# A decoder layer on one core: the norm's weight applied per partition behind the transposes, and four subtractions put behind the fifth product's addition

## The chip, the cores and the metric

The kernel runs on one core of a Trainium2 chip. It is one launch; the metric is the device time in microseconds of one execution, and of several executions the median counts. TensorE (PE in the profile) multiplies matrices, with its weight loads shown apart as PEld; VectorE is DVE, ScalarE is ACT, GpSimd is POOL, and SyncE is SP, which here issues nearly all DMAs. A line number such as L414 is a line of the kernel before. In the changed kernel the same statements stand a few lines further down.

## The reference

One layer of a decoder trunk over 1024 tokens of width 1024, in float32. Three parts follow each other, each adding to the residual stream `x`:

```python
def rms_norm(x, g):
    y = x * lax.rsqrt(jnp.mean(x * x, axis=-1, keepdims=True) + EPS)
    return y * g

def swiglu(h, w_gate, w_up, w_down):
    return (jax.nn.silu(h @ w_gate) * (h @ w_up)) @ w_down

x = x + 0.5 * swiglu(rms_norm(x, g_ffn1), w1_gate, w1_up, w1_down)    # hidden width 2816
h = rms_norm(x, g_mix)
proj = h @ w_in          # two token mixers with 8 heads of 64 each: sparse attention over the
...                      # top 256 keys with rotary positions, and stick-breaking attention
x = x + merged @ w_out
x = x + 0.5 * swiglu(rms_norm(x, g_ffn2), w2_gate, w2_up, w2_down)
```

The change is in how the two feed-forward parts (FFNs) get their normed input. `rms_norm` scales each row (token) by a number of its own and each column (feature) by `g`.

## The kernel before, in words

**Precision.** Every matrix product runs as three products of a reduced float32 type (fp32r): an operand is halved into a high part (a copy that rounds, on ScalarE, L377) and a low part (the operand less the high part, L378, on GpSimd or VectorE), and high times high, high times low and low times high are summed in PSUM. These are the matmul lines L497, L498 and L499 of an FFN's first half.

**An FFN's first half** (`ffn_in`) multiplies the normed input, as the right side, by gate and up weights, as the left side. It takes 2 by 2 blocks and a scheme with seven products in place of eight: the left sides are A11, A12, A22 and the sums S1 to S4, the right sides B11, B21, B22 and the sums T1 to T4 (each four tiles of 128x512 with its low halves beside it). T1 = B12 - B11, T2 = B22 - T1, T3 = B22 - B12, T4 = B21 - T2. Four banks of PSUM groups, with the letters a to d, take the products and the transposes in turn; a bank is free again when its last reader is done. The hidden width is walked in 11 pairs of blocks: the first pair by `opening`, all others by `products`. The second half (`ffn_out`) does the same with the down weights, and adds into `x`. FFN names begin with "a" in the first FFN, with "b" in the second.

**The right sides** are made by the class `Right`, the subject of the change. Its rows are the 128-token tiles of `x`, the first four (tokens 0 to 511) as one half, the last four as the other. `gain` loads `g` once, broadcast to all 128 partitions (128x1024). `stat` sums the squares of a tile on ScalarE (L408), computes the mean on VectorE (`ms`, L284) and the inverse root on GpSimd (`rs`, L286). `norm` multiplies a tile by `rs` (a value per partition) and by `g` (a value per column) in one VectorE instruction (L414), in two column halves for the first four tiles, whole for the last four. `turn` transposes the normed tiles on TensorE, four 128x128 pieces into a bank (L428), and halves the result from PSUM into a right side (ScalarE L377, VectorE L378); for B12 and B22 it also subtracts on VectorE to get T1, T3 and T2 (L431, L446). `keep` copies transposed values out of PSUM as they are, for later sums (L439 on VectorE, L441 on ScalarE), `less` subtracts lists (L446), and `low` halves T1 to T4 (L462 and L464).

**The order.** `opening` is written by hand: its instructions go to each engine in the order of the program. At its end stand, in this order, the sixth product into bank b, the halving of T3, `u2` plus that product (L617), four subtractions on VectorE for T4 (L446), the fifth product into bank d, `u3` = `u2` plus it (L622), the seventh product into bank c, the halving of T4, then the third product, which adds onto bank d, and the fourth onto bank c. Outside it a scheduler orders the instructions of each engine. In the second FFN the first two right sides are made while the output projection of the attention (`project`, matmul lines L308 to L310) still runs; it calls `between`, which turns B11 and B21. The attention in the middle is ordered by a planner of its own; the change does not alter that.

**The start.** SP issues the tiles x0 and x1, then `g`, x2 and x3, then the first gate weights `a0r` and up weights `a1r`. `gcolm`, a later load of another weight, already has the form that the change gives to `g`: eight rows of 128 are loaded, and turned into a value per partition and column tile.

Of the kernel before, what the change touches and what calls it, by code (L numbers as in the profile page):

```python
# [10 lines left out]
F32 = mybir.dt.float32  # L11
# [5 lines left out]
AF = mybir.ActivationFunctionType  # L17
ALU = mybir.AluOpType
# [5 lines left out]
P = 128  # L24
# [3 lines left out]
ND = D // P  # L28
# [3 lines left out]
HD = 64  # L32
# [25 lines left out]
def f32(ap):  # L58
    return ap.bitcast(F32)
# [186 lines left out]
def trunk(ctx, tc, x, positions, g_ffn1, w1_gate, w1_up, w1_down, g_mix, w_in, g_cq, w_uq_a, w_q_idx,  # L246
          g_q_a, g_k_a, w_uv_a, w_o_a, w_o_b, w_out, g_ffn2, w2_gate, w2_up, w2_down, inv_freq, out):
    nc = tc.nc
# [132 lines left out]
    class Right:  # L381
# [7 lines left out]
        def __init__(self, g, bank, gains, yt, ct, tt, ts, spare, nm):  # L389
            self.g, self.bank, self.gains, self.yt, self.ct = g, bank, gains, yt, ct  # L390
            self.tt, self.ts, self.spare, self.nm = tt, ts, spare, nm
            self.B, self.y, self.gB = {}, {}, None

        def gain(self):
            self.gB = self.gains(f"{self.nm}g")
            nc.sync.dma_start(self.gB, self.g[0].partition_broadcast(P))

        def place(self, xs, half, junk=None):

# [11 lines left out]
        def norm(self, t):  # L411
            xt = self.x[t]
            for c, out_ in ((slice(0, 1024), xt),) if self.half else ((HI, self.y[0, 0][t]), (LO, self.y[0, 1][t])):
                nc.vector.scalar_tensor_tensor(out_, xt[:, c], self.rs[t], self.gB[:, c], op0=ALU.mult, op1=ALU.mult)  # L414

        def operands(self, *ns):
            for n in ns:
# [2 lines left out]
        def turn(self, n, letters="abcd", less=None):  # L420

            if n not in self.B:
                self.operands(n)
            rows, out = self.y[self.ROWS[n]], []
            for k in range(4):
                ps = self.bank("pst", letters[k % len(letters)])
                for j in range(4):
                    nc.tensor.transpose(ps[:, j * P:(j + 1) * P], rows[j][:, k * P:(k + 1) * P], ident)  # L428
                halve(self.B[n][k], ps, nc.vector)
                if less:  # L430
                    nc.vector.tensor_sub(less[0][k], ps, less[1][k])  # L431
                out.append(ps)
            return out

        def keep(self, copies, eng=None):

            for t, ps in copies:
                if eng is nc.vector:
                    nc.vector.tensor_copy(t, ps)  # L439
                else:  # L440
                    nc.scalar.activation(t, ps, AF.Copy)  # L441

        def less(self, to, a, b):

            for t, p, q in zip(to, a, b):
                nc.vector.tensor_sub(t, p, q)  # L446

        def kept(self):

# [25 lines left out]
    def ffn_in(nm, R, wg, wu, raw, op, sums, ct, bank, staged, rows, first=None, beside=lambda n, ins: None):  # L475
# [54 lines left out]
        def opening(raws, rows, nxt):  # L530


            A = [dict(zip(("A11", "A12", "A21", "A22"), (r[:, q] for r in rs for q in (HI, LO)))) for rs in raws]
            O = ({}, {})

            def left(e, *names):
                for n in names:
                    O[e][n] = halve(op(f"{nm}{e}0{n}"), A[e][n])

            ps, sg = {}, {}  # L540

            def half(r, c, q, letter=None):

                if not q:
                    ps[r, c] = bank("pg", letter)
                times(O[0][f"A{r + 1}{q + 1}"], B[f"B{q + 1}{c + 1}"], ps[r, c], not q)

            def gate(r, c):
                sg[r, c] = ct(f"{nm}sg")
                nc.scalar.activation(sg[r, c], ps[r, c], AF.Silu)  # L550

            def up(n, ps_, start=True):
                a, b = FACTORS[n]
                times(O[1][a], B[b], ps_, start)

            if "B11" not in B:
                left(0, "A11")
                R.operands("B12", "B11", "B21", "B22", "T1")
                R.kept()
                copies = list(zip(R.raw["T3"], R.turn("B11")))  # L560
                left(0, "A12")
                R.keep(copies[0:1], nc.vector)
                p21 = R.turn("B21")
                R.kept2()
                copies += zip(R.raw["T4"], p21)
                left(0, "A21", "A22")
                R.second()
            else:
                copies = []
                R.operands("B22", "T1")  # L570
                left(0, "A11", "A12", "A21", "A22")
            for t, n in enumerate((("A11",), ("A12",), (), ())):
                R.keep(copies[1 + 2 * t:3 + 2 * t], nc.vector)
                if 4 - t <= len(rows):
                    R.stat(rows[t + len(rows) - 4])
                left(1, *n)
            r = R.raw
            r["T2"] = [R.spare(f"{nm}r22{k}") for k in range(4)]
            S = {n: sums(f"{nm}s{n}") for n in ("S1", "S2", "S3", "S4")}
            A11, A12, A21, A22 = (A[1][n] for n in ("A11", "A12", "A21", "A22"))  # L580
            nc.vector.tensor_add(S["S1"], A21, A22)
            nc.vector.tensor_sub(S["S2"], S["S1"], A11)
            A[1].update(S)
            for t in rows:
                R.norm(t)
            half(0, 0, 0, "a")
            half(0, 0, 1)
            gate(0, 0)
            left(1, "S2")
            half(1, 0, 0, "b")  # L590
            pa = bank("pa", "a")
            up(1, pa)
            u2 = ct(f"{nm}u2")
            half(1, 0, 1)
            nc.scalar.activation(u2, pa, AF.Copy)
            gate(1, 0)
            left(1, "S1")
            up(2, pa, False)
            R.turn("B12", "cdab", (r["T1"], r["T3"]))
            nc.gpsimd.tensor_sub(S["S3"], A11, A21)  # L600
            nc.gpsimd.tensor_sub(S["S4"], A12, S["S2"])
            left(1, "S3")
            R.less(r["T2"], R.turn("B22", "bcdc"), r["T1"])
            R.low("T1", nc.gpsimd)
            half(0, 1, 0, "d")
            half(1, 1, 0, "b")
            R.low("T2", nc.vector)
            left(1, "S4", "A22")
            half(0, 1, 1)
            gate(0, 1)  # L610
            half(1, 1, 1)
            gate(1, 1)
            R.less(r["T3"], r["T2"], r["T3"])
            pb = bank("pb", "b")
            up(6, pb)
            R.low("T3", nc.vector)
            nc.vector.tensor_add(u2, u2, pb)  # L617
            R.less(r["T4"], r["T4"], r["T2"])
            pd = bank("pd", "d")
            up(5, pd)  # L620
            u3 = ct(f"{nm}u3")
            nc.vector.tensor_add(u3, u2, pd)  # L622
            pc = bank("pc", "c")
            up(7, pc)
            R.low("T4", nc.vector)
            nc.vector.tensor_mul(sg[0, 0], sg[0, 0], pa)
            nc.vector.tensor_add(u3, u3, pc)
            nxt = nxt()
            up(3, pd, False)
            c12 = ct(f"{nm}c12")  # L630
            nc.vector.tensor_add(c12, u2, pd)
            up(4, pc, False)
            nc.vector.tensor_add(u2, u2, pc)
            return [sg[0, 0], sg[0, 1], sg[1, 0], sg[1, 1]], (None, c12, u2, u3), nxt
# [184 lines left out]
    with tc.tile_pool(name="ring1", bufs=1) as rpool, tc.tile_pool(name="s1", bufs=1) as spool, tc.tile_pool(name="ps1", bufs=1, space=PSUM) as psum:  # L819
# [3 lines left out]
        with tc.tile_pool(name="t1", bufs=1, side="right") as tpool, tc.tile_pool(name="c1", bufs=1) as cpool:  # L823
# [54 lines left out]
                rows(t)  # L878
            gcolm = column(g_mix, ND, "gcolm")
            gcolq = column(g_cq, QR // P, "gcolq")  # L880
            gk = cst.tile([P, HD], F32, name="gk")
            nc.sync.dma_start(gk, g_k_a[0].partition_broadcast(P))

            R.place(xs[0:4], 0)
            R.stat(0)
# [73 lines left out]
        h2, rows = [], []  # L959
# [68 lines left out]
    with ctxf, fp as fpool, psm as psum, tc.manual_schedule(  # L1028
# [384 lines left out]
        for w in ow.live:  # L1413
# [5 lines left out]
        rope, ropeq = s("rope", "rope", 2), s("ropeq", "rope", 2)  # L1419
        cos2, sin2, qcos, qsin = (t[:, j * 512:(j + 1) * 512].rearrange("p (t d) -> p t d", t=NT)  # L1420
                                  for t in (rope, ropeq) for j in range(2))
        cqh = [s(f"cqh{j}", "cqT", 4, F32R) for j in range(2)]
        cql = [s(f"cql{j}", "cqT", 4, F32R) for j in range(2)]
        KX, QI, WQ = {}, {}, {}
# [716 lines left out]
    with tc.tile_pool(name="ring2", bufs=1) as rpool, tc.tile_pool(name="ps6", bufs=1, space=PSUM) as psum:  # L2141
# [82 lines left out]
        with tc.tile_pool(name="c2", bufs=1) as cpool:  # L2224
            ct = of(cpool, "c", NC_, 512)
            x1 = residual(1)
            R = Right(g_ffn2, bank, fp(op), ct, ct, tt, ts, in_turn((sums, 3), (ct, 1)), "b")

            def between():
                R.operands("B12")  # L2230
                R.kept()
                R.kept2()
                R.keep(zip(R.raw["T3"], R.turn("B11")))
                R.keep(zip(R.raw["T4"], R.turn("B21")))

            R.gain()
            R.place(x0, 0)
            for t in range(4):
                R.stat(t)
                R.norm(t)  # L2240
            project(1, M1, x1, between)
            R.gain()
            R.place(x1, 1, sums)
            for t in range(3):
                R.stat(t)
                R.norm(t)

            ffn_in("b", R, w2_gate, w2_up, raw, op, sums, ct, bank, staged[1], [3])
# [51 lines left out]
```

## Time and profile before

| | us |
|---|---|
| median of 3 runs | 2156.49 (2155.02 to 2157.03) |
| the profiled execution's own time | 2154.83 |
| its span, first to last instruction | 2153.1 |
| TensorE busy | 2122.8 (99%) |
| VectorE busy | 1550.2 (72%) |
| ScalarE busy | 1041.4 (48%) |
| GpSimd busy | 907.1 (42%) |

The granted clock of TensorE was 1.000 over the span. The busy times overlap, since the engines work side by side; TensorE's idle time is the span less its busy time. A row of the timeline gives the start, the duration (of all instructions that the row groups, first start to last end), the engine, the line, the operation with its tiles (out<-in), the count, and in brackets the idle time of the engine ahead of it with what ended it. A row of the waits gives the total, the number and the longest of the waits of one line for another.

### The profile page before, as it was taken

What the parts mean: (1) busy time and instruction counts of PE and PEld (TensorE: products, weight loads), DVE (VectorE), ACT (ScalarE), POOL (GpSimd) and SP (SyncE); (2) the same over time, 40 slices, a digit from 0 to 9 for tenths busy, and PEclk for the clock granted to TensorE, in tenths of its full rate; (3) what the DMA queues carried; (4) which work ended last, traced back from release to release, by engine and by line L of the source; (5) the groups of instructions that cost most, each with busy time, mean ns of one, the idle gap of its engine ahead of it and who ended that gap; (6) DMA issues with size and microseconds to landing.
All of it is one profiled execution on the core that took longest, in us unless ns stands there. A gap on an engine that the chain in (4) does not pass through costs nothing. (4 is left out here: it accounts for less than half of the span.)

```text
span 2153.1 us, 30147 instructions
## 1 busy us (share of the span) xinstructions
PE 2122.8 (99%) x10308; PEld 1775.2 (82%) x10308; DVE 1550.2 (72%) x2618; ACT 1041.4 (48%) x1973; POOL 907.1 (42%) x732
## 2 busy tenths in 40 slices
PE   7999999999999999999999999999999999999999
PEld 6888888888889989788888888888888888888877
DVE  7776766688874499888885688864765646578685
ACT  6333343334455358987876566434532232324443
POOL 5554555523345444332211433244664555542223
PEclk9999999999999999999999999999999999999999
DMA  5587777497685342676744534465133323359655
GB/s 158 132 250 223 244 208 236 156 331 246 213 223 163 101 147 90 231 183 177 192 136 153 197 130 163 152 235 175 55 118 98 122 93 114 102 191 314 227 167 191
DMA packets 277979, 378.89 MB, mean 176 GB/s; under 512 B 39873, under 2 KB 165457, under 8 KB 277825
## 3 DMA queue, kind: packets, MB, share of 16 engines
q1 hardware_dynamic: 265792, 339.17, 50.6%
q0 software_dynamic: 12032, 37.79, 4.8%
q8 instruction: 81, 1.33, 0.3%
q14 instruction: 74, 0.60, 0.1%
HBM read 259.94 MB, written 116.95 MB: 175 GB/s over the span
## 5 line engine op out<-in xcount | busy, mean ns | idle before, releaser
L1286 ACT ACTIVATE junka<-u,cand,sig 128x768 bf16<-128x768 f32 (+1 forms) x124 | 134.4, 1084 | 3.8 <-DVE cand L1278 2.3
L859 ACT ACTIVATE swh<-swr 128x512 fp32r<-128x512 f32 x48 | 30.2, 630 | 120.1 <-issue 47.7
L1727 DVE TENSOR_TENSOR_SCAN left<-left 128x640 f32<-128x640 f32 (+3 forms) x64 | 86.8, 1372 | 1.1 <-ACT left L1721 1.0
L860 DVE TENSOR_TENSOR swr<-swr,swh 128x512 f32<-128x512 f32 x48 | 43.7, 910 | 46.4 <-ACT swh L859 44.1
L1785 DVE SCALAR_TENSOR_TENSOR pt<-pstT,pt 128x512 fp32r<-128x512 f32 (+1 forms) x96 | 51.6, 548 | 14.1 <-ACT pt L1782 13.7
L640 ACT ACTIVATE b0u<-b0u 128x512 f32<-128x512 f32 x20 | 12.7, 633 | 98.9 <-DVE b0u L520 82.9
L1788 DVE TENSOR_TENSOR pt<-pspT,pt 128x512 fp32r<-128x512 f32 x72 | 46.6, 684 | 17.5 <-ACT pt L1782 17.3
L1200 POOL DMA_DIRECT2D gd<-evg x32 | 18.6, 580 | 95.2 <-ACT evg L1195 92.8
L1782 ACT ACTIVATE pt<-pstT 128x512 fp32r<-128x512 f32 (+1 forms) x96 | 46.3, 492 | 24.1 <-PE pstT L1842 21.8
L1782 ACT ACTIVATE pt<-pspT 128x512 fp32r<-128x512 f32 x72 | 39.5, 596 | 32.7 <-PE pspT L2000 32.5
L1909 DVE CUSTOM_DVE_ANT_0 e<-psL,bias 128x512 f32<-128x512 f32 (+3 forms) x96 | 49.8, 551 | 7.2 <-PE psL L1946 7.1
L1921 ACT ACTIVATE e<-e,nm 128x768 f32<-128x768 f32 (+7 forms) x64 | 49.3, 775 | 10.5 <-DVE nm L1916 10.3
L737 PE MATMUL p<-aT,aS 128*128 128x512 f32 x132 | 51.6, 391 | 1.1 <-DVE aT L378 1.1
L737 PE MATMUL p<-bT,bS 128*128 128x512 f32 x132 | 51.6, 391 | 0.8 <-DVE bT L378 0.8
L1640 DVE SCALAR_TENSOR_TENSOR u<-relu,WI,u 128x512 f32<-128x512 f32 (+1 forms) x70 | 49.3, 723 | 3.7 <-ACT relu L1633 2.7
L738 PE MATMUL p<-aT,aS 128*128 128x512 f32 x132 | 50.7, 389 | 0.0
L1633 ACT ACTIVATE relu<-psdot 128x512 f32<-128x512 f32 (+1 forms) x80 | 39.7, 519 | 22.7 <-DVE u L1640 13.0
L738 PE MATMUL p<-bT,bS 128*128 128x512 f32 x132 | 50.4, 389 | 0.0
L736 PE MATMUL p<-bT,bS 128*128 128x512 f32 x132 | 47.0, 389 | 0.0
L1842 PE MATMUL pstT<-ident,left 128*128 128x128 f32 x288 | 45.9, 273 | 0.0
L377 ACT ACTIVATE bT<-bt 128x512 fp32r<-128x512 f32 x44 | 26.5, 625 | 39.6 <-PE p L738 32.2
L1721 ACT ACTIVATE left<-psz 128x512 f32<-128x512 f32 (+2 forms) x96 | 44.0, 500 | 2.5 <-PE psz L1750 2.1
(3046 smaller groups left out, 8210.9 us busy)
## 6 DMA issues: line engine op xcount, KB each, us to landing
aw<-in_w_down_dram SPq DMA_DIRECT2D x33, 512.0 KB, 4.9
bw<-in_w_down_dram SPq DMA_DIRECT2D x33, 512.0 KB, 5.0
swr<-in_w_in_dram SPq DMA_DIRECT2D x48, 256.0 KB, 6.2
a0r<-in_w_gate_dram SPq DMA_DIRECT2D x22, 512.0 KB, 8.0
a1r<-in_w_up_dram SPq DMA_DIRECT2D x22, 512.0 KB, 7.7
b0r<-in_w_gate_dram SPq DMA_DIRECT2D x22, 512.0 KB, 4.0
b1r<-in_w_up_dram SPq DMA_DIRECT2D x22, 512.0 KB, 3.8
x<-in_x_dram SPq DMA_DIRECT2D x16, 512.0 KB, 6.2
```

The lines of the kernel that those rows point to most:

```text
L736: nc.tensor.matmul(ps[q][m], S[:, h], T[:, HI], start=p == 0, stop=False)
L737: nc.tensor.matmul(ps[q][m], S[:, h], T[:, LO], start=False, stop=False)
L738: nc.tensor.matmul(ps[q][m], S[:, l], T[:, HI], start=False, stop=p == last)
L1286: nc.scalar.activation(junks[1][:, 0:(i + 1) * P], score[i], AF.Sign, scale=sig[:, b:b + 1], bias=cand.bitcast(F32)[:, b:b + 1], accum_out ...
L1640: nc.vector.scalar_tensor_tensor(ac, r, wv, ac, op0=ALU.mult, op1=ALU.add)
L1727: nc.vector.tensor_tensor_scan(back, back, back, 1.0, op0=ALU.mult, op1=ALU.bypass)
L1782: nc.scalar.activation(pt[:, off:512], tp[:, off:512], AF.Copy, bias=-less)
L1785: nc.vector.scalar_tensor_tensor(pt[:, 512 + off:1024], tp[:, off:512], -less, f32(pt[:, off:512]), op0=ALU.add, op1=ALU.subtract)
L1788: nc.vector.tensor_sub(pt[:, 512 + off:1024], tp[:, off:512], f32(pt[:, off:512]))
L1842: nc.tensor.transpose(tp[:, q * P:(q + 1) * P], A[n + q][:, j * P:(j + 1) * P], ident)
L1909: nc.vector.tensor_tensor_reduce(e[:, c], lp[:, 0:n_], bias[:, c], 1.0, LOW, op0=ALU.add, op1=ALU.max, accum_out=m)
L1921: nc.scalar.activation(e[:, 0:nk], e[:, 0:nk], AF.Exp, bias=nm_, accum_out=ssum)
```

## The change

`gain` now loads `g` as eight rows of 128 (4 KB), transposes them on TensorE into 128x8 in bank d (`psg`), and copies that to `gcol` on VectorE: one value per partition for each of the eight column tiles. `norm` multiplies by `rs` alone. What comes out of the transposes has features on partitions, so `g` is there a value per partition, and each reader of the bank multiplies by it: the high half and the copies on ScalarE as a scale, the low half and the subtractions on VectorE in an instruction that multiplies and subtracts (`scalar_tensor_tensor`), VectorE's copies as a `tensor_scalar`. Three other edits: the second FFN no longer loads `g` twice; in `opening`, the four subtractions for T4 stand behind `u3`; and `gk`, a 32 KB weight of the attention, is loaded at the attention's stage and not at the start.

```diff
         def gain(self):
-            self.gB = self.gains(f"{self.nm}g")
-            nc.sync.dma_start(self.gB, self.g[0].partition_broadcast(P))
+            rows = self.gains(f"{self.nm}g")[0:ND, 0:P]
+            nc.sync.dma_start(rows, self.g[0].rearrange("(k p) -> k p", p=P))
+            ps = self.bank("psg", "d")[:, 0:ND]
+            nc.tensor.transpose(ps, rows, ident[0:ND, 0:ND])
+            self.gcol = cst.tile([P, ND], F32, name=f"{self.nm}gcol")
+            nc.vector.tensor_copy(self.gcol, ps)
...
         def norm(self, t):
-                nc.vector.scalar_tensor_tensor(out_, xt[:, c], self.rs[t], self.gB[:, c], op0=ALU.mult, op1=ALU.mult)
+                nc.vector.tensor_scalar(out_, xt[:, c], self.rs[t], None, op0=ALU.mult)
...
         def turn(self, n, letters="abcd", less=None):
-                halve(self.B[n][k], ps, nc.vector)
+                at = 4 * self.ROWS[n][1] + k
+                ps = ps, self.gcol[:, at:at + 1]
+                t = self.B[n][k]
+                self.keep([(t[:, HI], ps)])
+                self.less([t[:, LO]], [ps], [f32(t[:, HI])])
                 if less:
-                    nc.vector.tensor_sub(less[0][k], ps, less[1][k])
+                    self.less(less[0][k:k + 1], [ps], less[1][k:k + 1])
...
         def keep(self, copies, eng=None):
-            for t, ps in copies:
+            for t, (ps, g) in copies:
                 if eng is nc.vector:
-                    nc.vector.tensor_copy(t, ps)
+                    nc.vector.tensor_scalar(t, ps, g, None, op0=ALU.mult)
                 else:
-                    nc.scalar.activation(t, ps, AF.Copy)
+                    nc.scalar.activation(t, ps, AF.Copy, scale=g)
...
         def less(self, to, a, b):
             for t, p, q in zip(to, a, b):
-                nc.vector.tensor_sub(t, p, q)
+                if isinstance(p, tuple):
+                    nc.vector.scalar_tensor_tensor(t, p[0], p[1], q, op0=ALU.mult, op1=ALU.subtract)
+                else:
+                    nc.vector.tensor_sub(t, p, q)
...
             nc.vector.tensor_add(u2, u2, pb)
-            R.less(r["T4"], r["T4"], r["T2"])
             pd = bank("pd", "d")
             up(5, pd)
             u3 = ct(f"{nm}u3")
             nc.vector.tensor_add(u3, u2, pd)
+            R.less(r["T4"], r["T4"], r["T2"])
...
-            gk = cst.tile([P, HD], F32, name="gk")
-            nc.sync.dma_start(gk, g_k_a[0].partition_broadcast(P))
...
+        gk = s("gk", "gk", 1, F32, (P, HD))
+        nc.sync.dma_start(gk, g_k_a[0].partition_broadcast(P))
...
             project(1, M1, x1, between)
-            R.gain()
             R.place(x1, 1, sums)
```

Of the order of the instructions, three places. The first is VectorE at the start, the norms of x0 and x1 (`ay00` and `ay10` are the two column halves of x0's normed tile; `ag` is `g`). Before:

```order
L284 TENSOR_SCALAR ms_230<-ss_228 128x1
L284 TENSOR_SCALAR ms_236<-ss_234 128x1
L414 SCALAR_TENSOR_TENSOR ay00_220<-x0_188,rs_232,ag_192 128x512
L414 SCALAR_TENSOR_TENSOR ay10_224<-x0_188,rs_232,ag_192 128x512
L414 SCALAR_TENSOR_TENSOR ay01_221<-x1_190,rs_238,ag_192 128x512
L414 SCALAR_TENSOR_TENSOR ay11_225<-x1_190,rs_238,ag_192 128x512
L284 TENSOR_SCALAR ms_244<-ss_242 128x1
```

And with the change:

```order
L284 TENSOR_SCALAR ms_232<-ss_230 128x1
L400 COPY agcol_196<-psg_194 128x8
L418 TENSOR_SCALAR ay00_222<-x0_188,rs_234 128x512
L418 TENSOR_SCALAR ay10_226<-x0_188,rs_234 128x512
L284 TENSOR_SCALAR ms_238<-ss_236 128x1
L418 TENSOR_SCALAR ay01_223<-x1_190,rs_240 128x512
L418 TENSOR_SCALAR ay11_227<-x1_190,rs_240 128x512
L284 TENSOR_SCALAR ms_246<-ss_244 128x1
```

The copy of `gcol` stands ahead of the first norm, and the mean of x1 stands behind the norms of x0, no longer ahead of them.

The second is VectorE near the end of `opening`, around the addition `u3`. Before:

```order
L464 TENSOR_TENSOR aT33_670<-araw3_288,aT33_670 128x512
L617 TENSOR_TENSOR au2_470<-au2_470,pb_654 128x512
L446 TENSOR_TENSOR ar210_349<-ar210_349,ar220_400 128x512
L446 TENSOR_TENSOR ar211_350<-ar211_350,ar221_401 128x512
L446 TENSOR_TENSOR ar212_351<-ar212_351,ar222_402 128x512
L446 TENSOR_TENSOR ar213_352<-ar213_352,ar223_403 128x512
L622 TENSOR_TENSOR au3_697<-au2_470,pd_684 128x512
L464 TENSOR_TENSOR aT40_712<-ar210_349,aT40_712 128x512
```

And with the change:

```order
L475 TENSOR_TENSOR aT33_672<-araw3_290,aT33_672 128x512
L628 TENSOR_TENSOR au2_472<-au2_472,pb_656 128x512
L632 TENSOR_TENSOR au3_695<-au2_472,pd_682 128x512
L457 TENSOR_TENSOR ar210_351<-ar210_351,ar220_402 128x512
L457 TENSOR_TENSOR ar211_352<-ar211_352,ar221_403 128x512
L457 TENSOR_TENSOR ar212_353<-ar212_353,ar222_404 128x512
L457 TENSOR_TENSOR ar213_354<-ar213_354,ar223_405 128x512
L475 TENSOR_TENSOR aT40_714<-ar210_351,aT40_714 128x512
```

The addition `u3` moved ahead of the four subtractions (`ar21` less `ar22`); the low halves of T4 stand behind all of them, as before.

The third is ScalarE in the second FFN, where B11 is made (`bB110` to `bB113`) behind the last weight conversion of the output projection. Before:

```order
L295 ACTIVATE wout116h_15220<-wout116r_15218 128x1024
L377 ACTIVATE bB110_15124<-pst_15128 128x512
L377 ACTIVATE bB111_15125<-pst_15135 128x512
L377 ACTIVATE bB112_15126<-pst_15142 128x512
L377 ACTIVATE bB113_15127<-pst_15149 128x512
L441 ACTIVATE braw0_15116<-pst_15128 128x512
```

And with the change:

```order
L295 ACTIVATE wout116h_15228<-wout116r_15226 128x1024
L377 ACTIVATE b00A11_15378<-b0r0_15360 128x512
L449 ACTIVATE bB110_15132<-pst_15136,bgcol_14946 128x512
L449 ACTIVATE bB111_15133<-pst_15143,bgcol_14946 128x512
L449 ACTIVATE bB112_15134<-pst_15150,bgcol_14946 128x512
L449 ACTIVATE bB113_15135<-pst_15157,bgcol_14946 128x512
L449 ACTIVATE braw0_15124<-pst_15136,bgcol_14946 128x512
```

The high half of the first gate weights (`b00A11`) now stands ahead of the high halves of B11, which take `gcol` as a scale.

More of the change, by code (lines that the diff above doesn't have):

```diff
@@ L391, in __init__ @@
             self.tt, self.ts, self.spare, self.nm = tt, ts, spare, nm
-            self.B, self.y, self.gB = {}, {}, None
+            self.B, self.y, self.gcol = {}, {}, None
         def gain(self):
-            self.gB = self.gains(f"{self.nm}g")
-            nc.sync.dma_start(self.gB, self.g[0].partition_broadcast(P))
+            rows = self.gains(f"{self.nm}g")[0:ND, 0:P]
[4 more added lines that the diff above has]
+            nc.vector.tensor_copy(self.gcol, ps)
         def place(self, xs, half, junk=None):
```

## The prediction

> **What bounds the kernel now.** I read the page first, then what TensorE waited for, then the timeline of the places that the change touches. First the page's busy times, then the view of the waits of TensorE (microseconds in total, how often, the longest).
>
> ```profile
> PE 2122.8 (99%) x10308; PEld 1775.2 (82%) x10308; DVE 1550.2 (72%) x2618; ACT 1041.4 (48%) x1973; POOL 907.1 (42%) x732
> ...
> PE pst L428 <- DVE ay L414: 13.9, 4, 8.6
> ...
> PE pd L497 <- DVE au L622: 0.8, 1, 0.8
> PE pd L497 <- DVE bu L622: 0.8, 1, 0.8
> ...
> PE pg L497 <- DVE araw L431: 0.2, 1, 0.2
> ```
>
> TensorE is busy for all but 30.3 us (2153.1 - 2122.8). The change removes no matmul, so it can win only from that idle time, or lose by adding to it. Three entries lie in lines that it edits: 13.9 us before the first transposes (8.6 us of it is the wait for the first normed rows), 0.8 us twice where the third product waits for `u3` (L622), and 0.2 us for a bank that L431 reads (the second FFN has the same again). VectorE at 72% and ScalarE at 48% are covered elsewhere, so a faster or slower instruction on them counts only at these places.
>
> **The start, where most of it is decided.** The timeline of the first 18 us; the bracket gives the idle time ahead and its releaser.
>
> ```profile
> 4.29 1.06 ACT L408 ACTIVATE ay<-x 128x1024 bf16<-128x1024 f32 x1 [2.27 <-DMA x<-in_x_dram]
> 5.60 1.06 ACT L408 ACTIVATE ay<-x 128x1024 bf16<-128x1024 f32 x1 [0.16 <-DMA x<-in_x_dram]
> 7.74 2.74 DVE L414 SCALAR_TENSOR_TENSOR ay<-x,rs,ag 128x512 f32<-128x512 f32 x4 [0.81 <-DMA ag<-in_g_ffn_dram]
> 8.90 1.06 ACT L408 ACTIVATE ay<-x 128x1024 bf16<-128x1024 f32 x1 [2.15 <-DMA x<-in_x_dram]
> 10.26 1.06 ACT L408 ACTIVATE ay<-x 128x1024 bf16<-128x1024 f32 x1 [0.20 <-DMA x<-in_x_dram]
> 11.21 1.42 DVE L414 SCALAR_TENSOR_TENSOR ay<-x,rs,ag 128x512 f32<-128x512 f32 x2 [0.66 <-POOL rs L286]
> 12.05 0.63 ACT L377 ACTIVATE a00A<-a0r 128x512 fp32r<-128x512 f32 x1 [0.65 <-DMA a0r<-in_w_gate_dram]
> 12.54 0.15 DVE L284 TENSOR_SCALAR ms<-ss 128x1 f32<-128x1 f32 x1
> 13.28 1.26 POOL L378 TENSOR_TENSOR a00A<-a0r,a00A 128x512 fp32r<-128x512 f32 x1
> 13.35 2.40 DVE L414 SCALAR_TENSOR_TENSOR ay<-x,rs,ag 128x512 f32<-128x512 f32 x2 [0.67 <-POOL rs L286]
> 15.23 3.00 PE L428 MATMUL pst<-ident,ay 128*128 128x128 f32 x13 [2.68 <-DVE ay L414]
> ...
> L414 DVE SCALAR_TENSOR_TENSOR ay<-x,rs,ag x8: 739/746/1740, 7.7 to 15.0; 128x512 f32<-128x512 f32 x8
> ```
>
> The reader sees three limits one behind the other: the broadcast g (512 KB, queued between x1 and x2) holds norm 0 until 7.74; x2 and x3 arrive late behind it (8.90, 10.26); and the last norm's first half takes 1.74 us, where the other norms take 0.75, beside GpSimd's subtraction of a00A, which ended at 14.54.
>
> **Term A, the start: -2.2.** The prices of what comes in place, from groups of the same operation elsewhere in this trace (min/median/max ns in the lines by source, busy us and mean ns in the groups):
>
> ```profile
> L1638 DVE TENSOR_SCALAR u<-relu,WI 128x512 f32<-128x512 f32 x6 | 2.9, 479 | 0.0
> L343 DVE TENSOR_SCALAR m1xn<-x,rs x4: 742/754/1633, 638.5 to 641.0; 128x1024 f32<-128x1024 f32 x4
> L359 DVE SCALAR_TENSOR_TENSOR mlo<-pst,gcolm,mhi x16: 735/742/751, 649.7 to 682.1; 128x512 fp32r<-128x512 f32 x16
> L378 DVE TENSOR_TENSOR aB<-pst,aB 128x512 fp32r<-128x512 f32 x16 | 10.5, 684 | 4.0 <-ACT aB L377 4.0
> L358 ACT ACTIVATE mhi<-pst,gcolm x16: 669/687/697, 648.7 to 681.4; 128x512 fp32r<-128x512 f32 x16
> L377 ACT ACTIVATE aB<-pst x16: 588/598/662, 15.7 to 41.4; 128x512 fp32r<-128x512 f32 x16
> ```
>
> So a norm of 512 columns falls from 0.746 to 0.479 us, a low half rises from 0.684 to 0.742 (+0.06), a high half from 0.60 to 0.687 (+0.085). Whole tiles of 512 KB arrived 1.31 and 1.36 us apart (4.29 to 5.60, 8.90 to 10.26). With 4 KB in g's place, x2 comes at 5.60 + 1.35 = 6.95, x3 at 8.3, and a0r 1.79 after it, as now, at 10.1. The eight rows of g come behind x1; I take 5.7, then a transpose of 0.45, the copy of 0.15 and the hand-overs, so norm 0 starts near 6.5 (now 7.74). The next tile's `ms` now stands behind the norms, not ahead of them: a tile is then two norms at 0.40 from start to start (0.479 less the 0.08 by which two neighbours overlap: 2 x 0.746 took 1.42), and 0.81 from `ms` to the norm behind it (12.54 to 13.35): 1.61 us, where it is now 2.14 (11.21 to 13.35). Norm 3 starts at 6.5 + 3 x 1.61 = 11.33; the sums of x2 and x3 (8.1, 9.5) are in time. GpSimd's a00A, its high half ready at 10.75, starts as the last `rs` ends, about 11.27, and ends at 12.5. It holds the last norm as now; what is left of that then takes some 0.4 us (now 0.55): 12.9, and the transposes resume at 13.05 in place of 15.23.
>
> That VectorE was stopped there by GpSimd is read from one row of 1740 ns among 746; the 1633 ns among 754 at L343 is the same with the very operation that is put in. By the section "The single rule" of the Trainium skill's page "SBUF — State Buffer", a VectorE operation with at most one SBUF input and outside its two-port modes does not contend with GpSimd; by that alone the new norm would go free. The 1633 speaks against it, and the same section lets a tensor_scalar enter a two-port mode.
>
> The bounds: if the loads come no sooner (x3 at 10.26), norm 3 cannot start before 12.4 and the gain is 0.7; if nothing holds the last norm, its first half ends at 11.8, TensorE resumes at 11.95, and it is 3.3.
>
> **Term C, the subtractions moved: -1.62.** The timeline before the third product:
>
> ```profile
> 57.01 0.39 PE L499 MATMUL pd<-aT,a10S 128*128 128x512 f32 x1
> 57.19 0.68 DVE L617 TENSOR_TENSOR au<-au,pb 128x512 f32<-128x512 f32 x1
> 57.78 2.49 DVE L446 TENSOR_TENSOR ar<-ar,ar 128x512 f32<-128x512 f32 x4
> 59.73 0.39 PE L499 MATMUL pc<-aT,a10S 128*128 128x512 f32 x1
> 60.19 0.68 DVE L622 TENSOR_TENSOR au<-au,pd 128x512 f32<-128x512 f32 x1
> 60.93 0.50 PE L497 MATMUL pd<-aB,a10S 128*128 128x512 f32 x1 [0.81 <-DVE au L622]
> 60.79 2.49 DVE L464 TENSOR_TENSOR aT<-ar,aT 128x512 fp32r<-128x512 f32 x4
> 66.89 0.39 PE L497 MATMUL pc<-aT,a10A 128*128 128x512 f32 x1
> ```
>
> The fifth product (`pd`) was done by 57.4 (57.01 + 0.39), but `u3` stood behind four subtractions and was added only at 60.19. Moved ahead of them it is done at 58.5, while TensorE still has the seventh product (`pc`) until 60.12. The 0.81 us go, once in each FFN: 1.62. What is late next is T4: its subtractions, high and low halves come some 0.6 us later. The low halves end now at 63.28 (60.79 + 2.49), and the fourth product that reads them begins at 66.89: covered. Bounds: 1.2 to 1.7.
>
> **The new prices at three seams, +1.2.** The first gate product reuses bank a:
>
> ```profile
> 19.51 0.68 DVE L439 COPY araw<-pst 128x512 f32<-128x512 f32 x1
> 20.47 0.47 PE L497 MATMUL pg<-aB,a00A 128*128 128x512 f32 x1
> 40.82 0.47 PE L497 MATMUL pg<-aB,a00A 128*128 128x512 f32 x1 [0.24 <-DVE araw L431]
> 1485.62 2.07 ACT L377 ACTIVATE bB<-pst 128x512 fp32r<-128x512 f32 x4 [5.00 <-PE pst L428]
> 1463.22 0.39 PE L308 MATMUL psout<-wout100h,m 128*128 128x512 f32 x1
> ```
>
> Bank a comes free at 20.19, 0.28 before its use. Ahead of it lie one high half and four low halves: 0.085 + 4 x 0.06 = 0.33, and the copy itself between 0.68 and 0.742; a stall of some 0.1 (0 to 0.3). At 40.82 TensorE waits already, so the same 0.33 shows in full, in both FFNs: +0.66 (0.3 to 0.8). In the second FFN ScalarE makes four high halves and the copy: 5 x 0.085, of which I put 0.35 on the path (0 to 0.8). There the transpose of g's rows is TensorE's, at 1463.22 between two row blocks of the output projection: +0.1 (0 to 0.45, one slow transpose). Together 0.1 + 0.66 + 0.35 + 0.1 = 1.2.
>
> **At nothing:** the second load of g (512 KB less beside matmuls that don't wait for it), the later load of `gk` (32 KB; behind it on SP's queue stand the loads of the attention's start, in a part of the order where the queue is not what comes last), the b00A high half now ahead of the first transposed halves on ScalarE (of the kind of the 0.63 at 12.05; ScalarE is idle for the 5.00 us ahead of 1485.62), and the work of the last FFN that stands in another order; that could move by what TensorE waits for there, 1 us either way.
>
> **Sum:** -2.2 - 1.62 + 1.2 = -2.6 against the profiled execution's 2154.83 (span 2153.1): 2152.2. The median shown, 2156.49, lies 1.66 above that execution, so the time is 2156.49 - 2.6 = 2153.9. A difference under 0.2% (4.3 us) can't be told from none by this measurement.
>
> **The rivals.** *The last norm goes free:* A is -3.3, and with a little less lost at the seams (0.8, bank a and the projection at nothing) the sum is -4.5: 2152.0. For it: a tensor_scalar reads one tensor, not two, and the order of the two starts (11.27 and 11.33) may turn round. Against: the 1633 at L343.
>
> *The load of g was not what held x2:* x2 waited 3.3 us behind x1, 2 us more than a tile, and that may be the queue's start-up. Then A is -0.7 and the sum -1.1: 2155.4; the change does not do what it says.
>
> *The slow transposes end at a fixed time.*
>
> ```profile
> L428 PE MATMUL pst<-ident,ay x32: 272/417/447, 8.6 to 20.4; 128*128 128x128 f32 x32
> L428 PE MATMUL pst<-ident,x x29: 270/273/273, 36.9 to 40.0; 128*128 128x128 f32 x29
> ```
>
> The first transposes take 417 ns, the later ones 273; from start to start that is 0.21 (13 in 3.00 us in the first timeline, less the last one's 0.45, by 12) against 0.11 (36.9 to 40.0 for 29). If that stretch ends at its own time (some 4 us after 15.23) and not so long after the start, 2.2 us of earlier transposes are worth about half: 1.1, and the sum is -1.5: 2155.0. The Trainium skill's page "TensorE: Matmul & The Clock Gate", section "What's actually happening", has such a rule: a free-running window of 3.4 us of steady work lifts the clock. It bears on this rival; the rows show the step, not what sets it.
>
> *The small load lands late, and the time is longer:*
>
> ```profile
> gcolm<-in_g_mix_dram SPq DMA_DIRECT2D x1, 4.0 KB, 8.2
> ag<-in_g_ffn_dram SPq DMA_DIRECT2D x1, 512.0 KB, 5.9
> ```
>
> The same shape of load (`gcolm`, eight rows of 128) took 8.2 us in a full queue, where the 512 KB took 5.9. Issued at 1.65 it lands at 9.85; norm 0 starts at 10.65, norm 3 at 15.5, where a00A's subtraction starts beside it as now; its first half ends near 17, 2 us later than now. With C and the seams the sum is 2.0 - 1.62 + 1.2 = +1.6: 2158.1. The start loses once the rows land after about 8.25 (A at nothing), the whole from 8.7 on, and by over 0.2% only with rows later than 12.5. Against it: `gcolm` stood behind six large loads, this behind two.
>
> **How the numbers follow.** Forecast 0.42, the free last norm 0.30, the loads not sooner 0.12, the fixed stretch 0.09, the late rows 0.07. The likeliest gives 2153.9. The range takes the free norm with 1.5 us for the last FFN's order (2150.5) and, above, the loads not sooner with 1.8 us for the seams' upper bounds and the median's own scatter (2157.2). Faster by over 0.2% (under 2152.2): 0.10 of the forecast and two thirds of the free norm, and a little for the last FFN: 0.27. Slower: 0.05, from the late rows and the last FFN. Within: 0.68.
>
> **What would show it.** Right: norm 0 at 6.3 to 6.8, x2's square sum near 7, the long pause before the thirteen transposes ending near 13; no wait of `pd` for L622 (now L632); the waits for L431's successor near 0.5. Wrong: x2 still at 8.9; the copy `agcol` (L400) after 8; the last norm's first half at 0.48; the transposes' slow stretch ending at 19 as now; TensorE waiting for T4 at the fourth product, or more than 2 us of new idle time in the second FFN.

## The result, and the profile after

The change made the kernel slower: 2178.06 us (median of 4 runs, 2176.50 to 2179.75) against 2155.76 for the kernel before beside it (4 runs). The ratio is 1.0103, with a 95% interval of 1.0086 to 1.0121: 22 us lost, where 2.6 us were forecast to be won and 2157.2 was the upper end of the range.

The page of the changed kernel, its busy times:

```profile
PE 2149.0 (99%) x10310; PEld 1777.0 (82%) x10310; DVE 1542.6 (71%) x2620; ACT 1045.4 (48%) x1973; POOL 913.9 (42%) x732
```

TensorE is busy 26.2 us longer than before (2122.8) with two instructions more, the small transposes of `g`. Its idle time is 29.0 us (2178.0 - 2149.0), before 30.3. So the time was not lost in a wait. The matmuls themselves stand further apart. The timeline by stages shows it in a stretch where no instruction was changed, and TensorE never stops. First before, then after (columns: stretch, its length, busy time of TensorE and its matmuls, granted clock, share of the DMA engines, GB/s):

```profile
100.00:400.00 300.00, 300.00 (x1325) 1.00 0.75 227
1700.00:1900.00 200.00, 200.00 (x884) 1.00 0.32 102
```

```profile
100.00:400.00 300.00, 300.00 (x1299) 1.00 0.74 225
1700.00:1900.00 200.00, 200.00 (x866) 1.00 0.31 99
```

In the same 300 us 1299 matmuls start in place of 1325, at the same granted clock: 231 ns from start to start (300 / 1299), not 226.4. That is two per cent on the distance of two starts. Over the 3720 matmuls of the first halves of the two FFNs it makes an estimated 17 us (4.5 ns each), most of the loss. The single matmuls of one block show that it is not spread evenly. The view of one tile (a02A, the left operands of the third block), before (min/median/max ns):

```profile
L497 PE MATMUL pa<-aB,a02A x8: 389/389/389, 105.0 to 117.9; 128*128 128x512 f32 x8
L498 PE MATMUL pa<-aB,a02A x8: 389/389/389, 105.2 to 118.1; 128*128 128x512 f32 x8
```

And after, with a08A (a left operand of a later block) behind it:

```profile
L508 PE MATMUL pa<-aB,a02A x8: 393/396/398, 103.8 to 117.0; 128*128 128x512 f32 x8
L509 PE MATMUL pa<-aB,a02A x8: 393/396/398, 104.0 to 117.2; 128*128 128x512 f32 x8
...
L508 PE MATMUL pa<-aB,a08A x8: 389/389/393, 337.0 to 350.2; 128*128 128x512 f32 x8
...
L508 PE MATMUL pc<-aT,a08A x4: 393/396/398, 350.9 to 353.0; 128*128 128x512 f32 x4
```

Before, every one takes 389. After, the first product (`pa`) with a02A takes 396, the one with a08A 389, and with a08A it is the fourth product (`pc`) that takes 396. The same operation on the same shapes goes at two speeds, and which tile goes at which changes from block to block.

The waits that the prediction spoke of, in the changed kernel:

```profile
PE psg L398 <- DMA ag<-in_g_ffn_dram: 5.5, 1, 5.5
PE pst L432 <- DVE ay L418: 3.5, 3, 1.2
PE p L748 <- DVE aT L378: 1.9, 1, 1.9
...
PE pa L510 <- POOL a01A L378: 1.5, 1, 1.5
PE pa L510 <- POOL b01A L378: 1.5, 1, 1.5
...
PE pg L508 <- ACT aB L449: 0.6, 1, 0.6
PE pg L508 <- ACT bB L449: 0.6, 1, 0.6
```

The wait for `u3` is gone. In its place stand 1.5 us in each FFN, where TensorE waits for a01A and b01A, the first left operand of the next block: a wait that did not stand among the waits before. The wait for bank d that stood against L431 (0.2 us in each FFN) is now 0.6 and stands against ScalarE's high half (L449).

### The profile page after: what moved, and what is told of

The parts are those of the page before. It is cut to its first block, busy times and chain, and to the rows that moved or that the text cites. A ratio compares the mean times of both kernels' runs of the same rounds, so it can differ in the third digit from the quotient of the medians.

```text
span 2178.0 us, 30148 instructions
## 1 busy us (share of the span) xinstructions
PE 2149.0 (99%) x10310; PEld 1777.0 (82%) x10310; DVE 1542.6 (71%) x2620; ACT 1045.4 (48%) x1973; POOL 913.9 (42%) x732
## 3 DMA queue, kind: packets, MB, share of 16 engines
q8 instruction: 81, 1.33, 0.2%
## 5 line engine op out<-in xcount | busy, mean ns | idle before, releaser
L748 PE MATMUL p<-aT,aS 128*128 128x512 f32 x132 | 52.4, 397 | 1.9 <-DVE aT L378 1.9
L749 PE MATMUL p<-aT,aS 128*128 128x512 f32 x132 | 51.8, 397 | 0.0
L747 PE MATMUL p<-aT,aS 128*128 128x512 f32 x132 | 45.9, 397 | 0.7 <-ACT aT L377 0.7
```

The source lines that it names most:

```text
L747: nc.tensor.matmul(ps[q][m], S[:, h], T[:, HI], start=p == 0, stop=False)
L748: nc.tensor.matmul(ps[q][m], S[:, h], T[:, LO], start=False, stop=False)
L749: nc.tensor.matmul(ps[q][m], S[:, l], T[:, HI], start=False, stop=p == last)
```

## The theories

The two speeds pointed at the tiles' places in the on-chip memory. The kernel takes its constants from a pool at the front of the left side, `cst`. The change puts `agcol` and `bgcol` (32 bytes of a partition each) into it and takes `gk` (256 bytes) out: 192 bytes less, and the left-hand pools behind it move down by 192. The right-hand pools stay. Tile starts by the program's own table of places, as the remainder by 256:

| tile | before | after |
|---|---|---|
| aB110, right operand (the columns that a matmul streams) | 192 | 192 |
| a02A11, left operand (the weights) of the first product with a02A | 192 | 0 |
| a08A11, the same with a08A, in a right pool | 192 | 192 |
| a08A22, left operand of the fourth product with a08A, in a left pool | 192 | 0 |

The two with 0 are the two that take 396 in the rows above. Before, of the 8172 matmuls with 512 reduced-float32 columns all but 48 have columns and weights that both start at 192. The source has two tiles that nothing reads, `edgel` (24 floats, at the front of `cst`) and `edger` (8 floats, at the front of the right side). They act as pads that bring both sides to this place. Matching the starts in the changed kernel's trace with this table, the matmuls whose columns stand at 192 and whose weights (their own and the next one's) at 0 follow each other after 233.4 ns on average (2294 of them); in the kernel before, with both at 192, it is 227.3 (7741 of them).

*Theory 1:* the place of the weights relative to the streamed columns sets the rate (1a), or the absolute place does (1b). *The rival:* the rate comes from the new instructions, the missing load, or the clock. A second question is kept apart: what the change would have brought with the places kept.

## Experiment 1: the places alone

The changed kernel, with the pad larger or smaller, and the kernel before, with nothing of the change but the pads (bytes are four times the floats). The order of the instructions is not altered by it on any engine. The two diffs below show only the lines that change.

```diff
-    cst.tile([P, 24], F32, name="edgel")
+    cst.tile([P, 72], F32, name="edgel")      # after_left192; after_left448: 8 floats
```

> The changed kernel with 192 bytes more of an unused pad at the front of the on-chip memory, so that every tile of the pools on the left side stands where it stood before the change; the order on all engines is the same as in the changed kernel. Theory 1 (place of the tiles): the 4 to 9 ns by which many 512-column matmuls start later in the changed kernel go, all FFN starts are 227 ns apart again, and some 24 of the 22 to 25 us come back: 2150 to 2157. Rival (the rate comes from the new instructions, from the missing load or from the clock): nothing changes, 2176 to 2180.

> The changed kernel with the pad 64 bytes smaller, so that the left pools stand 256 bytes below their place before the change. Theory 1 with a period of 256 bytes: as with 192 bytes more pad, 2150 to 2157, starts 227 ns apart. Theory 1 with a longer period, or with the absolute place: still slow, 2165 to 2185. Rival (not the place): 2176 to 2180.

```diff
-    ....tile([P, 8], F32, name="edger")
+    ....tile([P, 24], F32, name="edger")      # before_both_m64 only
-    cst.tile([P, 24], F32, name="edgel")
+    cst.tile([P, 8], F32, name="edgel")       # before_left_m64 and before_both_m64
```

> The kernel before, with nothing of the change, and only the pad 64 bytes smaller, so that left and right pools no longer have the same place within 256 bytes. Theory 1: slow without any of the change, 2165 to 2185, with starts of 231 and 236 ns where a left tile's weights meet a right tile's columns. Rival (the new instructions): 2155 to 2157.

> The kernel before with both sides' pools 64 bytes lower, so that left and right tiles keep the same place within 256 bytes relative to each other, at another absolute one (128 and not 192). Theory 1a (what counts is the weights' place relative to the moving operand's): as before, 2155 to 2157, 227 ns. Theory 1b (what counts is the absolute place, 192 within 256): slow, 2170 to 2190.

Three more distances followed, with `edgel` at 16 floats (before_left_m32), 40 (after_left64) and 48 (after_left96):

> The kernel before with the pad 32 bytes smaller, so that the left tiles stand 32 bytes lower within 256 than the right ones. If every difference of place costs (weights read beside columns of another place), some 5 to 25 us more, 2160 to 2180; if only steps of 64 bytes count, as before, 2155 to 2157.

> The changed kernel with 64 bytes more pad: the left tiles stand 128 bytes below their old place, half of 256 from the right ones. If the cost follows from weights and columns that differ in place within 256 bytes, whatever the distance: 2163 to 2178, with starts of over 230 ns where a left tile's weights meet a right tile's columns. If 128 bytes is a place where the two do not meet: 2150 to 2156.

> The changed kernel with 96 bytes more pad: the left tiles stand 96 bytes below their old place. As for 128 bytes below: 2163 to 2178 if every difference within 256 costs, 2150 to 2156 if this one does not.

Measured, with the left tiles' place less the right tiles', by 256, and the matmuls that start between 100 and 400 us of the trace:

| kernel | left less right | us | matmuls in 300 us |
|---|---|---|---|
| before | 0 | 2154.99 (15 runs) | 1325 |
| before_both_m64 | 0 (both at 128) | 2157.07 (1 run) | 1325 |
| after_left192 | 0 | 2152.13 (11 runs) | 1326 |
| after_left448 | -256 | 2151.45 (1 run) | 1325 |
| before_left_m32 | -32 | 2174.76 (1 run) | 1304 |
| before_left_m64 | -64 | 2166.39 (1 run) | 1318 |
| after_left96 | -96 | 2182.06 (1 run) | 1294 |
| after_left64 | -128 | 2176.99 (1 run) | 1299 |
| the change | -192 | 2178.06 (4 runs) | 1299 |

The time of the kernel before is the one beside after_left192, after_left448, before_left_m64 and before_both_m64; it took 2155.55 (27 runs) beside before_left_m32 and 2156.32 (1 run) beside after_left64 and after_left96. Six of the versions ran once. The four of them that are slower lose 11 us or more, where the 15 runs of the kernel before lie between 2153.55 and 2157.98, and the matmuls counted in 300 us of their traces tell the same.

The rival falls twice. The changed kernel with 48 unused floats more is 26 us faster than without, and the kernel before is 11 to 19 us slower with its pad alone made smaller. Theory 1b falls with before_both_m64: both sides at 128 is as good as both at 192. And 256 bytes of difference are none. So 1a holds in every run: what counts is the difference within 256 bytes. Each of the five differences tried costs, and not in order of size: 11 us at -64 against the kernel before, 30 at -96 against after_left192. Nor does its amount alone decide: -192, which within 256 is 64 the other way, costs 26. The branches that fell with it: a longer period than 256 bytes, steps of 64 that alone count, and 128 or 96 bytes as places where the two do not meet. For after_left96 the 2182 us lie above the span given (2163 to 2178). In before_left_m64 the time came out as expected, the two rates did not: where weights at 128 meet columns at 192 the starts are 229 ns apart on average, and 233 the other way round, not 231 and 236.

The loss can be placed as well. The changed kernel and after_left192 have the same matmuls in the same order, so their starts can be set against each other one by one, leaving out gaps of 300 ns and more. In the changed kernel they add up to 8.5 and 8.6 us more in the gate and up products of the two FFNs, 2.6 and 2.9 in the down products and 1.8 in the attention's output projection; all together it is 25.5 of the 25.9 us between the two times.

The same tile in before_left_m64, two of the three lines of the product slower, each by its own fixed amount:

```profile
L497 PE MATMUL pa<-aB,a02A x8: 392/392/392, 105.9 to 118.9; 128*128 128x512 f32 x8
L498 PE MATMUL pa<-aB,a02A x8: 394/394/394, 106.1 to 119.1; 128*128 128x512 f32 x8
L499 PE MATMUL pa<-aB,a02A x8: 388/388/389, 106.3 to 119.3; 128*128 128x512 f32 x8
```

And in after_left192, all back at 389:

```profile
L508 PE MATMUL pa<-aB,a02A x8: 389/389/389, 102.1 to 115.1; 128*128 128x512 f32 x8
...
L508 PE MATMUL pc<-aT,a08A x4: 389/389/389, 344.2 to 346.3; 128*128 128x512 f32 x4
```

What lies beneath is not shown. In these traces the load of the next weights overlaps the matmul before it (the load for the row at 64.01 us in the kernel before begins at 63.78, as the matmul ahead of it does), so it may be that these two reads get into each other's way when they stand at different places; no run took one of the two reads away. A neighbour that stands right is slowed as well for some six matmuls behind a wrong one: in the changed kernel's trace the matmuls with both at 192 average 229.2 ns, not 227.3; from the seventh on they stand at 226.7. So tiles at odds slow those beside them too.

## Experiment 2: the change with the places kept

With its tiles in their places the change gives about what was forecast: after_left192 against the kernel before beside it is 0.9985 (0.9976 to 0.9994), 3.2 us faster, between 1.3 and 5.2. But it is not made of the terms that the prediction had. The subtractions were taken alone, and taken out:

```diff
             nc.vector.tensor_add(u2, u2, pb)
-            R.less(r["T4"], r["T4"], r["T2"])
...
             nc.vector.tensor_add(u3, u2, pd)
+            R.less(r["T4"], r["T4"], r["T2"])
```

before_u3 is the kernel before with this and nothing else; after_left192_noU3 is after_left192 with this undone. In both the scheduler behind `opening` then also puts a few dozen matmuls of the next block in another order.

> The kernel before with only the four subtractions for T4 put behind the addition u3, in both FFNs; no tile changes its place. Theory by the prediction's term C: the 0.81 us in front of the third product go and nothing takes their place, -1.6 us in all. Rival, read from the changed kernel's waits: the subtractions feed T4's high halves on ScalarE, the next block's first high half (a01A) stands behind those, its low half on GpSimd behind that, and TensorE came to it with nothing to spare; there 0.75 of the 0.97 us per FFN are lost again, -0.4 us in all, no measurable difference, and TensorE waits 0.7 to 0.9 for a01A and for b01A.

> The changed kernel with the left pools at their place before the change (192 bytes more pad), and the four subtractions back ahead of u3: what is left is the norm weight per partition and the loads. By the rival above: as with the subtractions moved, within 1 us of 2152.1 less or more 0.4. By term C: 1.6 us more than that, 2153.8.

before_u3 took 2155.40 against 2155.55: 0.9997 (0.9988 to 1.0007), no difference that can be told. after_left192_noU3 took 2151.87, 0.9985 (0.9976 to 0.9994), the same as with the subtractions moved. The intervals alone would still leave room for 1.6 us; the traces do not. In before_u3 the wait for `u3` is gone and these came:

```profile
PE pa L499 <- POOL b01A L378: 1.4, 1, 1.4
PE pa L499 <- POOL a01A L378: 1.4, 1, 1.4
```

Matmul by matmul against the kernel before, the third product starts 0.97 us earlier, and 1.26 us are lost again before the third matmul with a01A (in the second FFN 0.94 and 1.33). The new waits are longer than the 0.7 to 0.9 expected. The chain is read in its timeline:

```profile
58.31 0.69 DVE L621 TENSOR_TENSOR au<-au,pd 128x512 f32<-128x512 f32 x1
58.92 2.49 DVE L446 TENSOR_TENSOR ar<-ar,ar 128x512 f32<-128x512 f32 x4
59.71 2.44 ACT L462 ACTIVATE aT<-ar 128x512 fp32r<-128x512 f32 x4 [3.79 <-DVE ar L446]
62.06 0.61 ACT L377 ACTIVATE a01A<-a0r 128x512 fp32r<-128x512 f32 x1
62.75 2.20 POOL L378 TENSOR_TENSOR a01A<-a0r,a01A 128x512 fp32r<-128x512 f32 x1 [9.90 <-ACT a01A L377]
...
65.00 0.50 PE L499 MATMUL pa<-aB,a01A 128*128 128x512 f32 x1 [1.36 <-POOL a01A L378]
```

VectorE's subtractions release T4's high halves on ScalarE one by one, and behind these, in ScalarE's order, stands the high half of a01A, whose low half GpSimd makes next (it ends at 64.95, and TensorE goes on at 65.00). In the kernel before, GpSimd's row and those of TensorE's second and third matmul of that block are:

```profile
61.62 2.82 POOL L378 TENSOR_TENSOR a01A<-a0r,a01A 128x512 fp32r<-128x512 f32 x1 [9.12 <-ACT a01A L377]
64.01 0.39 PE L498 MATMUL pa<-aB,a01A 128*128 128x512 f32 x1
64.49 0.50 PE L499 MATMUL pa<-aB,a01A 128*128 128x512 f32 x1
```

0.48 us from start to start where 0.23 is usual, and GpSimd's row ends at 64.44: TensorE waited there already. The chain through ScalarE and GpSimd was the next bound, with nothing to spare.

To test the chain, a01A's high half was put ahead of T4's (not shown here: the helper that makes the left sides of a block in two steps):

```diff
             up(7, pc)
+            nxt = nxt()            # loads the next block, halves its A11 (a01A); returns the rest
             R.low("T4", nc.vector)
...
             nxt = nxt()            # the sums and the other halves, as before
```

> The changed kernel with 192 bytes more pad, and in the opening the first high half of the next block (a01A, b01A) put ahead of T4's four high halves on ScalarE, its low half with it on GpSimd. By the chain named for the subtractions: TensorE's waits of 0.8 for a01A and b01A go, 1.6 us less than with the pad alone, about 2150.5. If something else holds that product: no difference, 2152.1.

The waits for a01A and b01A are gone from its trace, which was expected, and at the fourth product TensorE is 3.9 us ahead of the kernel before (62.98 for the row that stands at 66.89 there), against 2.8 in after_left192:

```profile
62.98 0.45 PE L516 MATMUL pc<-aT,a10A 128*128 128x512 f32 x1
```

That bears out the chain as what held that product. But the edit did one thing more: with a01A early, the scheduler put eleven of its twelve matmuls ahead of the third product, so that product no longer follows the seventh at once, and what each of the two did is not told apart. And only 0.3 us of the lead lasts: by 102 us the lead is 3.1, against 2.8. One more wait took its place:

```profile
PE pc L516 <- DVE a0u L536: 0.4, 1, 0.4
```

Here TensorE reaches the next block's products before VectorE has emptied their bank. It took 2151.26 us, 0.9980 (0.9971 to 0.9989): 0.2% faster than the kernel before. Its lead over after_left192 (0.9985) lies within the intervals of both; the 1.6 us expected did not come.

## Why the prediction was wrong, point by point

**The step that failed** is the sentence that the whole sum stands on, that a change which removes no matmul "can win only from that idle time, or lose by adding to it", and with it the list "At nothing". TensorE's idle time fell from 30.3 to 29.0 us; it was its busy time, taken as fixed, that rose by 26.2, since the same matmuls stood further apart. The load of `gk` elsewhere and `gcol` in its place were looked at as instructions, waits and queue positions, and hidden as such; after_left192, which has them all, is not slower for them. They were not priced as bytes in a pool that stands in front of others. Those 192 bytes cost some 26 us (2178.06 less 2152.13), ten times the sum of all terms. No rival had it either: all were about the order and the length of waits. (One of their sums is also off: for the last norm going free, -3.3 - 1.62 + 0.8 is -4.1, not -4.5.) What could have been read: the sum of the tiles that the diff adds to and takes from `cst`, and the two unread pad tiles in the source.

**Term A, the start: -2.2 forecast, -2.9 to -3.2 and then -2.5 to -2.8 measured.** From after_left192, whose start is that of the change with the places kept:

```profile
10.08 0.88 DVE L418 TENSOR_SCALAR ay<-x,rs 128x512 f32<-128x512 f32 x2 [0.66 <-POOL rs L286]
10.88 0.15 DVE L284 TENSOR_SCALAR ms<-ss 128x1 f32<-128x1 f32 x1
11.69 1.91 DVE L418 TENSOR_SCALAR ay<-x,rs 128x512 f32<-128x512 f32 x2 [0.66 <-POOL rs L286]
11.93 1.38 POOL L378 TENSOR_TENSOR a00A<-a0r,a00A 128x512 fp32r<-128x512 f32 x1 [0.28 <-ACT a00A L377]
12.32 4.86 PE L432 MATMUL pst<-ident,ay 128*128 128x128 f32 x24 [1.16 <-DVE ay L418]
```

The first norm starts at 6.50, and a tile takes 1.61 us (10.08 to 11.69), both as worked out. The last norm starts at 11.69 where 11.33 was forecast, since x2 came sooner by less than the forecast said: its square sum begins at 8.08 here and at 7.43 in the changed kernel, where 8.90 stood before and 6.95 was forecast. So the load of `g` did hold x2, and that rival fell.

The transposes resume at 12.32, not 13.05, since the last norm's first half went free: it started before GpSimd's subtraction and took 0.49 us, which the prediction had named as a sign of being wrong. The second half, which started behind the subtraction, was held instead (1.91 for two that take 0.88 elsewhere, 1.50 for the second alone). That is the first rival, on its second ground: the one operation went free or was held with the order of the two starts, and that it reads one tensor did not set it free.

The rival of the fixed slow stretch fell. The transposes drop from some 420 ns to 273 at 19.7 us in the kernel before and between 16.6 and 17.6 in the four versions with the places kept: the slow stretch moved with the transposes. It lasted 4.3 to 5.3 us from where they resume, before 4.4, and the longer ones are most of what is lost again of the 2.9 to 3.2 us before the first gate product, where 2.5 to 2.8 are left. The small load was early: TensorE took it up at 5.5 in the changed kernel and at 6.1 in after_left192 (5.7 forecast), and the rival of the late rows fell.

**Term C: -1.62 forecast, nothing measured.** "Covered" was checked for T4's own reader, the fourth product. The block behind it on ScalarE was not looked at.

**The seams: 1.2 forecast, 1.4 measured** from the traces matmul by matmul (after_left192_noU3): bank a 0.0 (0.1 forecast), bank d 0.33 in each FFN (0.33), the first transposed halves of the second FFN 0.33 (0.35), and the transpose of `g` there 0.42 (0.1). This was the best part. The wait for bank d is 0.6 in all (0.24 + 0.33), near the 0.5 that the prediction named.

**The sum.** -2.5 to -2.8 at the start, 1.4 at the seams, and in the last FFN, whose order the scheduler changed, 1.5 to 2.1 us less between 2070 and 2104, where two waits of 0.8 and 0.2 stood before: -2.6 to -3.5, against -3.2 (-5.2 to -1.3) by the times. The single traces of the four versions end between 1.1 us behind the kernel before's and 3.4 ahead, since the waits in the second half of the first FFN and at its seam to the attention differ from one to the next by more than a microsecond. So the forecast of -2.6 holds for the change without its shift of the tiles, but by luck in its parts: C's gain is missing, and the last FFN's, which was put at "1 us either way", stands in its stead.

## What to carry to other kernels

Sum the bytes that a change adds to and takes from every pool that stands ahead of others, and compare the remainder by 256 of the tiles that meet in a matmul before anything is said of its time; here a pad of 48 more floats restored it. When TensorE is busy longer with the same instructions, look at the distance of starts tile by tile before looking for a wait. And when an instruction is moved behind another, follow not only its own readers but what stands behind those readers on their engine.

## What was not expected of the hardware

In this kernel the rate of the reduced-float32 matmuls of 512 columns depends on where weights and columns lie relative to each other within 256 bytes: 227.3 ns from start to start when all have the same place, otherwise between 227 and 236 on average, by which places meet and which matmuls stand beside; 11 to 30 us of 2155. In two of the traces of the changed kernel and its variants TensorE's granted clock fell to 0.5 for 3.4 us inside the run, after TensorE had waited 0.7 and 1.9 us in quick succession in one, and 2.6 us in the other (after_left192, at 702 us). What sets it was not tested. From the changed kernel (the last row is of the stretches: busy time and count of TensorE, its weight loads, VectorE, ScalarE and GpSimd, then the granted clock, the DMA share and GB/s):

```profile
633.48 0.50 PE L748 MATMUL p<-aT,aS 128*128 128x512 f32 x1 [1.91 <-DVE aT L378]
...
634.20 0.63 PE L748 MATMUL p<-aT,aS 128*128 128x512 f32 x1
634.63 0.63 PE L749 MATMUL p<-aT,aS 128*128 128x512 f32 x1
...
634.00:637.00 3.00, 3.00 (x8) 2.32 (x8) 3.00 (x3) 1.62 (x3) 2.26 (x2) 0.50 0.68 221
```

There a matmul starts every 0.43 us and not every 0.23, which makes this wait an estimated 1.6 us dearer than it reads (8 matmuls by 0.2).
